# Weight sums of a decoder layer: their transfers on ScalarE's queue, in groups of half-size tiles

## The chip, the cores and the metric

The kernel runs on one core of one Trainium2 chip. The metric is the device time of one execution in microseconds (us). The kernel before took 1721.75 us in the median of three runs (1721.25 to 1722.3).

The engines are named as in the profile: PE is TensorE, DVE is VectorE, ACT is ScalarE, POOL is GpSimd, SP is SyncE. SP does no arithmetic here; it issues transfers, and "SP's queue" is the order in which it issues them. Every engine works through its own instructions in order, and a transfer that an engine issues is one of them.

## The reference, cut to what matters

One decoder layer in float32 with 1024 tokens: two mixers side by side, an output projection, a gated feed-forward network, and a gated embedding at the end.

```python
def forgetting_attention(q, k, v, f_logit, f_bias, q_gain, k_gain):
    ...
    c = jnp.cumsum(logf, axis=1).transpose(0, 2, 1)
    for blk in range(S // FOX_BLOCK):
        ...
        s = jnp.einsum('bhtd,bhsd->bhts', qh[:, :, t0:t1], kh[:, :, :t1]) * scale
        s = s + c[:, :, t0:t1, None] - c[:, :, None, :t1]
        ...
        pr = jax.nn.softmax(s, axis=-1).astype(vh.dtype)
        outs.append(jnp.einsum('bhts,bhsd->bhtd', pr, vh[:, :, :t1]))
...
        x = x + (jax.nn.silu(hf @ w_ffn_gate[layer]) * (hf @ w_ffn_up[layer])) @ w_ffn_down[layer]
```

Two parts matter here: the attention, eight heads of width 64, and the last product, whose weights `w_ffn_down` have 2816 x 1024 elements.

## The kernel before, in words

The stages follow one another: the first mixer (to about 375 us), the attention (about 380 to 760 us), the projections that merge both, the feed-forward network, and the embedding. Float32 products are made of three matmuls each, of a rounded high part and the rest (`xhi`, `xlo`, `whi`, `wlo`; lines 156 to 158 for one shape, 402 to 404 for another).

The attention goes over four pairs of heads, numbered 0 to 3 here, one call of `fox_mix(pr)` each. A pair has two halves. In the first, 24 **score blocks** (two heads, rows in blocks of 128, one or two column ranges) are computed only to find each row's maximum (the reduction of line 871 on DVE). The maxima are transposed on PE (line 879), split into `uh` and `ul` on DVE (lines 882 and 883), and four transfers of line 886 write them into rows 66 to 69 of the operand `QA`. In the second half the scores are computed again with these rows in the contraction, so that they come out with the maximum already subtracted: line 912 on PE needs the transfers of line 886. Then come the exponential on ACT (line 919), its split into `ph` on POOL (line 923) and `pl` on DVE (line 924), and the products with the values. Where the attention leaves PE free, `fill(n)` issues matmuls of projections that are needed later; their results leave PSUM by line 644 on ACT, with line 657 (a square) on ACT, lines 658 to 660 on DVE, line 661 (a power) on POOL, line 666 (the scaling) on DVE and line 669 (the store `qd`) on SP.

The down projection is computed with seven products of sums of blocks in place of eight products of blocks, so it needs four sums of blocks of `w_ffn_down` (S1 to S4) for each of its 11 steps `kp`. `down_sums()` makes these during the attention: for each `kp` it loads four blocks of 128 x 512 (line 789), forms four sums on POOL (line 795), each in the place of one of its operands, and stores them to the DRAM tile `sd` (line 797), from which the down projection loads them much later. `down_sums()` is a generator; `fox_mix` advances it by one step after every score block (line 874), 96 steps in all, so that pairs 0 to 2 have three `kp` each and pair 3 has two. Loads and stores both stand in SP's queue (`dma` is `nc.sync.dma_start`); the tiles come from the pool `wsum` with six buffers.

```python
t[n] = wsum.tile([P, HALF], F32, tag="sw", name="sw")
after_anchor(dma(t[n], wts[U_DOWN + 2 * kp + i][:, b * HALF:(b + 1) * HALF]))
...
    after_anchor(ptt(t[z], t[x], t[y], op))
    yield
    after_anchor(dma(sd[n, kp], t[z]))
```

The order on PE is that of the code. The order on the other engines is set by a scheduler when the program is built; `after_anchor` tells it to place an instruction no earlier than the latest score matmul, which adds no wait on the chip. Transfers report on eight counters in turn (DMAHW0 to DMAHW7): a transfer that takes a counter waits until the one that had it has landed, whichever queue that was issued from.

Of the kernel before, what the change touches and what calls it, by code (L numbers as in the profile page):

```python
# [9 lines left out]
F32 = mybir.dt.float32  # L10
# [4 lines left out]
ALU = mybir.AluOpType  # L15
# [4 lines left out]
P = 128  # L20
# [3 lines left out]
HALF = 512  # L24
D_FF = 2816
NFF = D_FF // P
NPAIR = NFF // 2
# [17 lines left out]
U_DOWN = U_UP + NFF  # L45
# [18 lines left out]
def layer(ctx, tc, xT, pT, wts, wf_in, consts, masks, outT):  # L64
    nc = tc.nc
    dma = nc.sync.dma_start
# [71 lines left out]
    for n, m in GATES_BEFORE:  # L138
        i = order.index(n)
# [145 lines left out]
    for c in range(8):  # L285
        t = w2() if c < 4 else hg.tile([P, HALF], F32, tag=("Kt", "Qt")[c % 2], name="vraw")
# [466 lines left out]
    fstack = ExitStack()  # L753
# [15 lines left out]


    sd = dram.tile([4, NPAIR, P, HALF], F32, name="sd")
    wsum = fstack.enter_context(tc.tile_pool(name="wsum", bufs=6, reuse_waits="tile"))
    S2, S3, S4, S1 = range(4)

    anchor = [None]
# [1 line left out]
    def after_anchor(ins):  # L777

        tc.add_manual_dep(ins.ins, anchor[0].ins.name,
                          mybir.DependencyInfo(mybir.DependencyClass.NoSync,  # L780
                                               mybir.DependencyReason.DATA), reason="order")

    def down_sums():

        for kp in range(NPAIR):
            t = {}
            for n, (i, b) in (("21", (0, 1)), ("22", (1, 1)), ("11", (0, 0)), ("12", (1, 0))):
                t[n] = wsum.tile([P, HALF], F32, tag="sw", name="sw")
                after_anchor(dma(t[n], wts[U_DOWN + 2 * kp + i][:, b * HALF:(b + 1) * HALF]))
            yield  # L790
            yield
            yield
            for x, y, z, op, n in (("21", "22", "22", ALU.add, S1), ("11", "21", "21", ALU.subtract, S3),
                                   ("22", "11", "11", ALU.subtract, S2), ("12", "11", "12", ALU.subtract, S4)):
                after_anchor(ptt(t[z], t[x], t[y], op))  # L795
                yield
                after_anchor(dma(sd[n, kp], t[z]))
            yield

    wsums = down_sums()  # L800
    staged = {}

# [261 lines left out]
    op = ostack.enter_context(tc.tile_pool(name="op", bufs=3, side="right", reuse_waits="tile"))  # L1064
# [267 lines left out]
    for n, (p, kp) in enumerate(todo):  # L1332
# [7 lines left out]
        if n == 2:  # L1340
# [4 lines left out]
                                                 reuse_waits="tile"))  # L1345
# [9 lines left out]
        _, _, g, begin, into, done = products[p]  # L1355
# [129 lines left out]
```

## Time and profile before

| | |
|---|---|
| runs, median (lowest to highest) | 1721.75 us (1721.25 to 1722.3) |
| profiled execution | 1719.14 us, span 1717.4 us |
| PE busy | 1618.3 us, 94% of the span |
| DVE busy | 1088.9 us, 63% |
| ACT busy | 638.7 us, 37% |
| POOL busy | 596.1 us, 35% |
| chain that ended last | PE 85%, DMA 3%, POOL 3%, DVE 3% |
| DMA | 223.45 MB, mean 130 GB/s |

The busy shares are means over all stages. Issuing a transfer is not counted as busy time; in a timeline, SPq is SP's queue, and the time beside an instruction of it is what the issuing took. A releaser (behind "<-") is the event that ended an engine's idle time. PEclk is the clock that TensorE was granted, 1.00 for the full 2.4 GHz and 0.50 for half of it.

### The profile page before, as it was taken

Reading aid. Unit: us, or ns where it says so; the run is one execution under the profiler, and the core shown is the slowest. Engines: PE = TensorE matmul, PEld = TensorE weight load, DVE = VectorE, ACT = ScalarE, POOL = GpSimd, SP = SyncE. Lnnn points to the kernel's source line nnn. Section 1 sums busy time; section 2 is a strip of 40 time slices with the busy share of each in tenths; the row PEclk is TensorE's granted clock in tenths of the full one; section 3 lists DMA queues with packets and bytes.
Section 4 is the critical chain, followed back from the end, with each engine's and each line's share of the span. In section 5 each row is a group of like instructions: output and inputs, shape, how many; then the busy total and the mean of one; then the engine's idle time right before and its main releaser. Section 6 shows DMA issues by size and latency. Waiting matters only on the chain.

```text
span 1717.4 us, 21469 instructions
## 1 busy us (share of the span) xinstructions
PE 1618.3 (94%) x8086; PEld 1356.8 (79%) x8086; DVE 1088.9 (63%) x1431; ACT 638.7 (37%) x888; POOL 596.1 (35%) x452
## 2 busy tenths in 40 slices
PE   8999999997694969799999999999999999999998
PEld 6889889997583847577888888888888878888887
DVE  7457776755462636556547777777777757657442
ACT  7244655632221304156224433333333334445310
POOL 2243444423315233231213466656665620102200
PEclk9999999999796989899999999999999999999999
DMA  5332211246556373707224332223322278665111
GB/s 203 99 113 72 74 62 51 87 139 175 168 146 200 101 227 106 213 33 271 69 101 150 126 104 105 93 92 123 114 96 92 92 253 302 199 193 187 61 64 47
DMA packets 120615, 223.45 MB, mean 130 GB/s; under 512 B 14368, under 2 KB 43424, under 8 KB 120512
## 3 DMA queue, kind: packets, MB, share of 16 engines
q1 hardware_dynamic: 120512, 222.09, 39.4%
q8 instruction: 63, 1.03, 0.2%
q14 instruction: 40, 0.33, 0.1%
HBM read 148.25 MB, written 61.15 MB: 122 GB/s over the span
## 4 chain that ended last, share of the span: by engine, by line
PE 85%; DMA 3%; POOL 3%; DVE 3%; issue 2%; ACT 2%; SPq 1%; POOLq 0%; DVEq 0%; ACTq 0%
PE ps_z L156 14%; PE ps_z L157 14%; PE ps_z L158 14%; PE ps_m L156 6%; PE ps_m L158 6%; PE ps_m L157 6%; POOL sw L795 3%; PE ps_z L402 2%; PE ps_z L403 2%; PE ps_z L404 2%; DMA sw<-wts 1%; PE ps_m L488 1%; PE ps_a L158 1%; PE ps_a L157 1%; PE ps_a L156 1%
## 5 line engine op out<-in xcount | busy, mean ns | idle before, releaser
L156 PE MATMUL ps_z<-xhi,whi 128*128 128x512 f32 x624 | 254.8, 408 | 0.7 <-ACT xhi L173 0.7
L157 PE MATMUL ps_z<-xlo,whi 128*128 128x512 f32 x624 | 245.5, 393 | 0.6 <-DVE xlo L176 0.6
L158 PE MATMUL ps_z<-xhi,wlo 128*128 128x512 f32 x624 | 245.0, 393 | 0.0
L924 DVE TENSOR_TENSOR pl<-p,ph 128x512 fp32r<-128x512 f32 (+3 forms) x96 | 55.4, 583 | 130.7 <-POOL ph L923 130.2
L158 PEld LDWEIGHTS ps_z<-xhi,wlo 128*128 128x128 f32 x624 | 118.1, 189 | 25.2
L1082 DVE TENSOR_TENSOR wlo<-dr,whi 128x1024 fp32r<-128x1024 f32 x75 | 94.9, 1267 | 66.5 <-ACT whi L1081 65.8
L156 PEld LDWEIGHTS ps_z<-xhi,whi 128*128 128x128 f32 x624 | 119.5, 192 | 21.7 <-ACT xhi L173 1.1
L157 PEld LDWEIGHTS ps_z<-xlo,whi 128*128 128x128 f32 x624 | 118.6, 190 | 22.7 <-DVE xlo L176 2.4
L128 ACT CAST whi<-raw 128x1024 fp32r<-128x1024 f32 (+1 forms) x69 | 72.4, 1049 | 153.9 <-PE ps_z L157 119.2
L1081 ACT CAST whi<-dr 128x1024 fp32r<-128x1024 f32 x75 | 79.1, 1055 | 108.7 <-PE ps_m L158 90.0
L129 DVE TENSOR_TENSOR wlo<-raw,whi 128x1024 fp32r<-128x1024 f32 (+1 forms) x69 | 101.6, 1472 | 28.3 <-ACT whi L128 23.8
L402 PE MATMUL ps_z<-whi,xhi 128*128 128x256 f32 (+1 forms) x384 | 112.8, 294 | 0.0
L912 PE MATMUL ps_m<-QA,KA 68*128 68x512 f32 (+3 forms) x96 | 36.2, 377 | 77.0 <-DMA QA<-ul 76.8
L403 PE MATMUL ps_z<-wlo,xhi 128*128 128x256 f32 (+1 forms) x384 | 108.6, 283 | 0.0
L404 PE MATMUL ps_z<-whi,xlo 128*128 128x256 f32 (+1 forms) x384 | 108.5, 283 | 0.0
L919 ACT ACTIVATE p<-ps_m 128x512 f32<-128x512 f32 (+3 forms) x96 | 46.3, 491 | 157.9 <-PE ps_m L915 137.7
L1275 POOL TENSOR_TENSOR w<-w,rb 128x512 f32<-128x512 f32 x44 | 63.0, 1433 | 103.1 <-ACT w L1274 103.1
L923 POOL TENSOR_SCALAR ph<-p 128x512 fp32r<-128x512 f32 (+3 forms) x96 | 53.3, 559 | 126.5 <-ACT p L919 126.4
L1304 POOL TENSOR_TENSOR acc<-acc,o 128x512 f32<-128x512 f32 x14 | 24.6, 1756 | 190.8 <-ACT o L1303 190.1
L795 POOL TENSOR_TENSOR sw<-sw 128x512 f32<-128x512 f32 x44 | 58.3, 1324 | 81.4 <-DMA sw<-wts 78.8
L912 PEld LDWEIGHTS ps_m<-QA,KA 68*128 68x128 f32 x96 | 19.3, 201 | 82.3 <-DMA QA<-uh 54.6
L403 PEld LDWEIGHTS ps_z<-wlo,xhi 128*128 128x128 f32 x384 | 73.3, 191 | 0.7
(462 smaller groups left out, 4518.2 us busy)
## 6 DMA issues: line engine op xcount, KB each, us to landing
raw<-wts SPq DMA_DIRECT2D x71, 512.0 KB
hb<-w SPq DMA_DIRECT2D x77, 256.0 KB
dr<-hb SPq DMA_DIRECT2D x75, 256.0 KB
sw<-wts SPq DMA_DIRECT2D x44, 256.0 KB
sd<-sw SPq DMA_DIRECT2D x44, 256.0 KB
rg<-wts SPq DMA_DIRECT2D x22, 512.0 KB
ru<-wts SPq DMA_DIRECT2D x22, 512.0 KB
dr<-sd SPq DMA_DIRECT2D x44, 256.0 KB
```

What stands on the lines that cost most here:

```text
L128: nc.scalar.copy(hi, raw)
L129: tt(lo, raw, hi.bitcast(F32), ALU.subtract)
L156: mm(ps, w[0], x[0], start=first, stop=False, skip_group_check=more)
L157: mm(ps, w[0], x[1], start=False, stop=False, skip_group_check=more)
L158: mm(ps, w[1], x[0], start=False, stop=last, skip_group_check=more)
L402: mm(ps[:, off:off + n], xh[:, cs], hi, start=k == 0, stop=False)
L403: mm(ps[:, off:off + n], xh[:, cs], lo, start=False, stop=False)
L404: mm(ps[:, off:off + n], xl[:, cs], hi, start=False, stop=k == KT - 1)
L795: after_anchor(ptt(t[z], t[x], t[y], op))
L1081: nc.scalar.copy(hi, src)
L1082: tt(lo, src, hi.bitcast(F32), ALU.subtract)
L1275: ptt(s, s, hv(rb, h), ALU.mult)
```

## The change

Loads and stores of the sums are issued by ACT (`sdma` is `nc.scalar.dma_start`). The work is cut into 22 groups, two for each `kp`, of tiles of 128 x 256 in place of 128 x 512. The pool has twelve such buffers in place of six large ones, the same bytes. Loads of group g + 1 and stores of group g - 1 stand ahead of the sums of group g in the code. 44 loads, 44 sums and 44 stores become 88 of each, all of half the size: 176 transfers of 128 KB in ACT's queue for 88 of 256 KB in SP's.

```diff
-    wsum = fstack.enter_context(tc.tile_pool(name="wsum", bufs=6, reuse_waits="tile"))
+    wsum = fstack.enter_context(tc.tile_pool(name="wsum", bufs=12, reuse_waits="tile"))
...
+    sdma = nc.scalar.dma_start
+    groups = [(kp, q) for kp in range(NPAIR) for q in range(2)]
+
+    def sum_load(kp, q):
+        t = {}
+        for n, (i, b) in (("21", (0, 1)), ("22", (1, 1)), ("11", (0, 0)), ("12", (1, 0))):
+            t[n] = wsum.tile([P, 256], F32, tag="sw", name="sw")
+            c = b * HALF + q * 256
+            after_anchor(sdma(t[n], wts[U_DOWN + 2 * kp + i][:, c:c + 256]))
+        return t
+
     def down_sums():
-        for kp in range(NPAIR):
-            t = {}
-            for n, (i, b) in (("21", (0, 1)), ("22", (1, 1)), ("11", (0, 0)), ("12", (1, 0))):
-                t[n] = wsum.tile([P, HALF], F32, tag="sw", name="sw")
-                after_anchor(dma(t[n], wts[U_DOWN + 2 * kp + i][:, b * HALF:(b + 1) * HALF]))
-            yield
-            yield
-            yield
-            for x, y, z, op, n in (("21", "22", "22", ALU.add, S1), ("11", "21", "21", ALU.subtract, S3),
-                                   ("22", "11", "11", ALU.subtract, S2), ("12", "11", "12", ALU.subtract, S4)):
-                after_anchor(ptt(t[z], t[x], t[y], op))
-                yield
-                after_anchor(dma(sd[n, kp], t[z]))
-            yield
+        t, done = sum_load(*groups[0]), []
+        for _ in range(4):
+            yield
+        for g, (kp, q) in enumerate(groups):
+            for dst, src in done:
+                after_anchor(sdma(dst, src))
+            ahead = sum_load(*groups[g + 1]) if g + 1 < len(groups) else None
+            done = []
+            for x, y, z, op, n in (("21", "22", "22", ALU.add, S1),
+                                   ("11", "21", "21", ALU.subtract, S3),
+                                   ("22", "11", "11", ALU.subtract, S2),
+                                   ("12", "11", "12", ALU.subtract, S4)):
+                after_anchor(ptt(t[z], t[x], t[y], op))
+                done.append((sd[n, kp][:, q * 256:(q + 1) * 256], t[z]))
                 yield
-                after_anchor(dma(sd[n, kp], t[z]))
-            yield
+            t = ahead
+        yield
+        for dst, src in done:
+            after_anchor(sdma(dst, src))
```

In the changed file the load is line 791, the sum line 808, the store line 801 (the last group's line 814); every line from 799 on of the kernel before has moved down by 16, so lines 879, 886, 912, 919 and 923 are lines 895, 902, 928, 935 and 939 there.

The built program shows how the other instructions move. SP's queue at the end of pair 0's first half, before (`raw` is a weight for a projection, `VL`, `zt` and `qd` are the attention's own tiles, and DVE_49, Pool_49 and Activation_49 are waits for those engines):

```order
L789 DMA sw<-wts 128x512 [waits DMAHW3_49,DMAHW0_49]
L669 DMA qd<-zn 128x4x128 [waits DMAHW1_49,DVE_49,Activation_49]
L797 DMA sd<-sw 128x512 [waits Pool_49] x2
L669 DMA qd<-zn 128x4x128 [waits DMAHW4_49]
L797 DMA sd<-sw 128x512 [waits DMAHW5_49,Pool_49]
L797 DMA sd<-sw 128x512 [waits DMAHW6_49,Pool_49]
L886 DMA QA<-uh 1x8x128 [waits DMAHW7_49,DVE_49]
L886 DMA QA<-ul 1x8x128 [waits DMAHW0_49,DVE_49]
L886 DMA QA<-uh 1x8x128 [waits DMAHW1_49]
L886 DMA QA<-ul 1x8x128 [waits DMAHW2_49]
```

The same place after:

```order
L862 DMA VL<-vfd 128x64 [waits DMAHW1_49]
L863 DMA VL<-vfd 128x64 [waits DMAHW3_49]
L864 DMA VL<-vfd 128x7x128 [waits DMAHW5_49]
L669 DMA qd<-zn 128x4x128 [waits DMAHW0_49,DVE_49,Activation_49]
L669 DMA qd<-zn 128x4x128 [waits DMAHW3_49]
L117 DMA raw<-wts 128x1024 [waits DMAHW6_49]
L902 DMA QA<-uh 1x8x128 [waits DMAHW4_49,DVE_49]
L902 DMA QA<-ul 1x8x128 [waits DMAHW1_49,DVE_49]
L902 DMA QA<-uh 1x8x128 [waits DMAHW2_49]
L902 DMA QA<-ul 1x8x128 [waits DMAHW3_49]
```

The stores and loads of the sums no longer stand ahead of the four `QA` transfers. These now come behind two `qd` stores, and wait for counters that were last taken by transfers of ACT's queue: in pair 0 by a load of group 4 and by stores of group 3. In pair 1 they wait likewise for a store of group 8 and a load of group 10; in pair 2 for the second store of group 14, and, through the `raw` load ahead of them, for a load of group 15; in pair 3 for the last store of group 20 and two stores of group 21.

ACT's order from pair 0's first score blocks to its first exponential (line 919), before:

```order
L644 ACTIVATE zn<-ps_z,r_539 128x256 x2
L657 ACTIVATE w_3755<-zn 128x512
L644 ACTIVATE zn<-ps_z,r_539 128x256 x2
L657 ACTIVATE w_3760<-zn 128x512
L644 ACTIVATE zn<-ps_z,r_539 128x256 x2
L657 ACTIVATE w_3962<-zn 128x512
L128 CAST whi<-raw 128x1024
L644 ACTIVATE zn<-ps_z,r_539 128x256 x2
L657 ACTIVATE w_3967<-zn 128x512
L919 ACT_TABLE_LOAD
L919 ACTIVATE p<-ps_m 128x512 x2
```

The same place after, from the second pair of `zn` on, where the exponential is line 935:

```order
L801 DMA sd<-sw 128x256
L657 ACTIVATE w_3771<-zn 128x512
L801 DMA sd<-sw 128x256 x3
L791 DMA sw<-wts 128x256 x4
L801 DMA sd<-sw 128x256 x4
L791 DMA sw<-wts 128x256 x4
L801 DMA sd<-sw 128x256 x4
L791 DMA sw<-wts 128x256 x4
L644 ACTIVATE zn<-ps_z,r_539 128x256 x2
L128 CAST whi<-raw 128x1024
L644 ACTIVATE zn<-ps_z,r_539 128x256 x2
L657 ACTIVATE w_3998<-zn 128x512
```

Before these rows stand 16 more transfers, behind the first pair of `zn` and its square. The third and fourth pairs of `zn`, their squares and a cast of weights (line 128) now stand behind all the transfers of the pair, with the exponential behind them. 40, 48, 48 and 40 transfers stand ahead of the first exponential of pairs 0 to 3. POOL has 20, 24, 24 and 20 half-size sums there, where it had 12, 12, 12 and 8 full ones. In pair 0 its order was two of line 661, one of line 661, four sums, one of line 661, eight sums; it is now one of line 661, twelve sums, one of line 661, eight sums, two of line 661.

## Rows read from the trace of the kernel before

**Rows 1.** Waits of PE, 380 to 780 us; us in total, times, longest.

```profile
PE ps_m L912 <- DMA QA<-ul: 76.8, 4, 23.6
```

**Rows 2.** Timeline of PE: L912's first matmul of each pair; in brackets, idle before.

```profile
443.01 0.80 PE L912 MATMUL ps_m<-QA,KA 68*128 68x512 f32 x1 [23.33 <-DMA QA<-ul]
...
547.32 0.77 PE L912 MATMUL ps_m<-QA,KA 68*128 68x512 f32 x1 [23.62 <-DMA QA<-ul]
...
646.69 0.77 PE L912 MATMUL ps_m<-QA,KA 68*128 68x512 f32 x1 [19.36 <-DMA QA<-ul]
...
727.11 0.77 PE L912 MATMUL ps_m<-QA,KA 68*128 68x512 f32 x1 [10.44 <-DMA QA<-ul]
```

**Rows 3.** Waits of SP's DMA queue, 380 to 780 us; columns as in 1.

```profile
SPq L797 <- POOL sw L795: 92.0, 44, 13.0
```

**Rows 4.** Chain of work, 414 to 444 us; start us, us, what.

```profile
421.57 3.65 DMA sw<-wts
...
441.19 1.77 DMA QA<-ul
```

**Rows 5.** Tile sw: its lines; ns min/median/max, first and last start in us.

```profile
L789 SPq DMA_DIRECT2D sw<-wts x44: 375/426/1067, 400.4 to 714.9; - x44
L795 POOL TENSOR_TENSOR sw<-sw x44: 1259/1262/2147, 414.6 to 722.7; 128x512 f32<-128x512 f32 x44
L797 SPq DMA_DIRECT2D sd<-sw x44: 319/320/744, 415.9 to 723.9; - x44
```

**Rows 6.** Timeline of POOL in pairs 0, 1 and 2; start us, us, instruction.

```profile
395.47 1.64 POOL L661 TENSOR_TENSOR r<-ss,cf 128x8 f32<-128x8 f32 x1 [16.16 <-DVE ss L660]
...
425.35 5.28 POOL L795 TENSOR_TENSOR sw<-sw 128x512 f32<-128x512 f32 x4 [2.57 <-DMA sw<-wts]
434.63 5.28 POOL L795 TENSOR_TENSOR sw<-sw 128x512 f32<-128x512 f32 x4 [3.99 <-DMA sw<-wts]
...
499.47 1.65 POOL L661 TENSOR_TENSOR r<-ss,cf 128x8 f32<-128x8 f32 x1 [13.23 <-DVE ss L660]
...
627.52 5.28 POOL L795 TENSOR_TENSOR sw<-sw 128x512 f32<-128x512 f32 x4 [5.90 <-DMA sw<-wts]
638.24 5.28 POOL L795 TENSOR_TENSOR sw<-sw 128x512 f32<-128x512 f32 x4 [5.44 <-DMA sw<-wts]
```

**Rows 7.** Timeline of SP's queue, pair 0's end and pair 2's start.

```profile
440.35 0.75 SPq L886 DMA_DIRECT2D QA<-uh  x1
...
442.58 0.63 SPq L886 DMA_DIRECT2D QA<-ul  x1
...
599.66 1.24 SPq L840 DMA_DIRECT2D KB<-zt  x1
```

**Rows 8.** Timeline of ACT in pairs 0, 2 and 3.

```profile
416.29 0.84 ACT L644 ACTIVATE zn<-ps_z,r 128x256 f32<-128x256 f32 x2 [0.38 <-PE ps_z L404]
...
595.46 1.05 ACT L128 CAST whi<-raw 128x1024 fp32r<-128x1024 f32 x1 [1.58 <-PE ps_z L157]
...
686.02 0.58 ACT L942 COPY w<-ps_a 64x512 f32<-64x512 f32 x1
```

**Rows 9.** Groups of POOL by form, 380 to 740 us; busy us, mean ns, idle before.

```profile
L923 POOL TENSOR_SCALAR ph<-p 128x512 fp32r<-128x512 f32 x38 | 25.5, 676 | 64.9 <-ACT p L919 64.9
...
L923 POOL TENSOR_SCALAR ph<-p 128x256 fp32r<-128x256 f32 x14 | 6.0, 432 | 12.8 <-ACT p L919 12.8
```

**Rows 10.** Stretches behind the four stops; PEclk is the granted clock.

```profile
443.00:447.20 4.20, 4.19 (x11) 2.77 (x12) 0.69 (x1) 1.02 (x2) 0.62 (x1) 0.50 0.65 182
...
727.10:730.50 3.40, 3.39 (x9) 2.07 (x10) 0.00 (x0) 1.88 (x2) 0.01 (x1) 0.50 0.65 222
sum 18.60, PE 18.56 PEld 12.20 DVE 2.82 ACT 6.22 POOL 3.10; mean PE 4.64 PEld 3.05 DVE 0.70 ACT 1.56 POOL 0.77
```

**Rows 11.** Timeline of DVE around pair 0's stop.

```profile
422.82 0.69 DVE L666 TENSOR_TENSOR zn<-zn,r 128x512 f32<-128x512 f32 x1 [2.95 <-POOL r L661]
...
445.73 0.69 DVE L924 TENSOR_TENSOR pl<-p,ph 128x512 fp32r<-128x512 f32 x1 [22.22 <-POOL ph L923]
```

## The prediction

> **What bounds the kernel now.** The waits of PE come first. PE is busy nearly all the time, so a change elsewhere can only give back time in which PE stands. In the attention stage almost all such time has one cause: four stops, one per pair of heads, at the first score matmul of the second half (line 912), which waits for the maxima to be written into QA. They make 76.8 us [rows 1]. PE's timeline shows each: the idle time in brackets, taken from the start beside it, gives PE's arrival at 419.7, 523.7, 627.3 and 716.7 us [rows 2].
>
> Next, why QA is late. The waits of SP's queue show the store of a sum waiting for POOL 44 times, 92.0 us in all [rows 3]. The QA transfers are issued only at 440.35 in pair 0 [rows 7], though the engine that makes their data (DVE) had been idle for 22 us when it next worked [rows 11]. They stand in SP's queue behind all sums of the pair, and these run in a closed circle: the chain shows a load landing 3.65 us after its issue [rows 4], then four sums of 1.26 us each and four stores [rows 5], and only then the next loads. POOL's timeline gives the length of a circle: 9.28 us in pair 0 (425.35 to 434.63) and 10.72 in pair 2 (627.52 to 638.24) [rows 6]. So the place to look at is the interval from a pair's start to its QA transfers, not POOL's or ACT's share of the span.
>
> The stops cost more than their length. In the stretches behind them the granted clock reads 0.50, which is 1.2 GHz, for 18.6 us of PE work in the four of them together (the first, the last and the sum of four stand in [rows 10]); at 1.00 that work would take half. So 9.3 us more hang on the stops, and 86.1 us can be had at most.
>
> **The change part by part.** *Removed from SP's queue:* 88 issues and the head-of-line wait. If nothing new came in, all 86.1 us would go. What is late next is the new wait of QA for counters held by ACT's transfers, so that chain has to be worked out.
>
> *A half sum.* No row shows one. The nearest is the same engine's copy: 676 ns for 512 columns, 432 for 256 [rows 9], so 188 of it is fixed. With that, 1262 ns [rows 5] becomes 188 + 537 = 0.72 us; I take 0.70. Bounds are half (0.63) and no saving (1.26). Eighty-eight at 0.70 are 61.6 us for today's 44 x 1.32 = 58.3: 3 us more on POOL, under other work.
>
> *The period of a group.* POOL alone would allow 4 x 0.70 = 2.8 us, the lower bound. With loads one group ahead, the loads of g + 1 follow the last store of g - 1: one store issue of 0.32, four load issues of 0.43 [rows 5], a landing of 3.65 [rows 4] and the sums of 2.8 make 8.5 us for two groups, 4.2 each. Half of today's circle, 4.6 us in pairs 0 and 1 and 5.4 in pairs 2 and 3, is near that and holds the load of the other transfers, so I take it. The upper bound is a full trip per group, without overlap: 3.65 + 0.32 + 2.8 = 6.8.
>
> *When QA can be written.* Behind the last sum stand a store's landing, taken as 2.0 us (bounds 1.77 and 3.65, the two landings of rows 4), and the QA transfers, 440.35 to 442.96, 2.6 us [rows 4, 7].
> - Pair 0 needs group 3 stored. POOL is free at 395.47 + 1.64 = 397.1 [rows 6]; 397.1 + 4 x 4.6 + 1.65 for a line 661 in between + 4.6 = 421.8. PE is there at 419.7: 2 us.
> - Pair 1 needs group 8 stored, and group 5 is loaded already: 499.47 + 1.65 = 501.1, + 3 x 4.6 + 1.65 + 4.6 = 521.2 against 523.7. The load of group 10 also gates and comes up to 4 later; I take 1 us.
> - Pair 2 starts when ACT has done its cast, 595.46 + 1.05 = 596.5 [rows 8]: four loads and their landing 5.4, sums 2.8, two periods 10.8, 4.6 make 620.1; through the load of group 15 it is a period and a landing more, 629. PE comes at 627.3; I take 2.
> - Pair 3 starts at 686.02 + 0.58 = 686.6 [rows 8] and has five groups: 686.6 + 5 x 5.4 + 4.6 = 718.2 against 716.7; I take 2.
>
> Left of the waits: 7 us (bounds 0 and 28, the latter by the period of 6.8).
>
> *Behind the wait.* ACT now evicts two quarters of a projection (twice 0.84, twice a square) and makes a cast of 1.05 [rows 8] between the pair's last transfer and its first exponential, and POOL has eight half sums and line 661 twice ahead of `ph`. That was done during the wait before. I take 4 us for pair 0 and 5 for pair 1, none for pairs 2 and 3, where no quarters stand: 9 (bounds 0 and 16, twice 8).
>
> *In the scoring half.* Line 661 on POOL now has up to twelve half sums ahead of it, and DVE's line 666 waits for it; today that wait is 2.95 us [rows 11]. Evictions on ACT wait behind stores that wait for POOL. I take 3 us for each pair, 12 (bounds 0 and 24).
>
> *SP's other transfers* now share counters with ACT's. An issue that is held up takes 1.24 us where others take 0.63 [rows 7]; one late landing is 3.65. I take 1.5 us for each pair, 6 (bounds 0 and 14.6).
>
> *ACT's issuing.* 176 issues. The trace has none on ACT; SP's take 0.32 to 0.43 in the median [rows 5], and the longest near row is 1.24 [rows 7]. I take 0.37, so 40 to 48 of them are 15 to 18 us per pair in stretches of 24 to 31 us (worked out below): no term of its own, because ACT otherwise waits for PE there. If that cover is gone the second rival applies.
>
> *The clock.* Shorter stops remain; I leave half of the 9.3 us lost, 4.7 (bounds 0 and 9.3).
>
> **Sum.** 86.1 - (7 + 9 + 12 + 6 + 4.7) = 47.4 us gained. The profiled execution took 1719.14 us, 2.6 below the median of the runs, so 1671.7 in its terms and **1674 us** in the runs'. All bounds at once would give 1635 (nothing left of the losses) and 1727 (28 + 16 + 24 + 14.6 + 9.3 = 91.9 in place of 38.7). They will hardly all fall to one side, so the likeliest case's own range goes half way to each, 1655 to 1700.
>
> **The rivals.**
> - *The full trip stays.* Stores wait at the head of ACT's queue, ahead of the next loads, so nothing overlaps and a period is 6.8 us. Pair 0 waits 2 + 4 x 2.2 = 11, pair 1 about 4, pair 2 about 4, pair 3 2 + 5 x 1.4 = 9, 28 instead of 7; 4.6 of clock is lost too. That gives about 1700. For it: today's circle is exactly this. Against: twelve buffers are three groups, so the loads of g + 1 need the buffers of g - 2, not of g - 1.
> - *ACT's queue becomes the bound*, on the slow side. Place: the transfers ahead of the first exponential of each pair. From the pairs' starts (395.47 and 499.47 by rows 6, 596.5 and 686.6) to PE's arrivals there are 24 + 24 + 31 + 30 = 109 us. With x us per issue ACT needs 176 x there, and 2 x 0.84 + 1.05 = 2.7 us per pair of evictions and a cast, 11 in all; with 12 us of stalls in scoring it breaks even with the 76.8 of today at x = (109 + 76.8 - 11 - 12) / 176 = 0.92. At 1.0 the kernel is 0.08 x 176 = 14 us slower, **1736 us**. For it: waits for POOL and for counters now lie on an engine that evicts PE's banks, and an issue was seen to take 1.24 when held up. Against: the medians of SP are 0.32 and 0.43, less than half of that point.
> - *Nearly all comes back.* The period is POOL's 2.8 and no stall of scoring appears: only about 7 us are left of the 86.1, so 1719.1 - 79 + 2.6 = 1642.
> - *No change.* Moving transfers between queues does nothing, because the transfers themselves are the limit, and QA is as late as before: 1721. The row that speaks against it is the 92.0 us of a queue's head waiting for POOL, not for a transfer [rows 3]. The Trainium skill says it in "DMA: Bandwidth & Descriptors", section "Issuing engines are not separate DMA queues": transfers of several engines run on the same 16 DMA engines, and issuing from several saves only the sequencer's time to initiate, usually small. By that rule the result would be this rival's; the trace agrees with it on the data's path but shows what it leaves out, a queue whose head waits.
>
> **How the numbers follow.** The forecast gets 0.56, the full trip 0.13, nearly all 0.11, no change 0.05, ACT's queue 0.15. The range leaves out the last two: from 1640 (nearly all) to 1706 (the full trip, with 6 us for its waits). A measurement of this kernel can tell about 0.2%, 3.4 us, from no change. Faster: 0.56 + 0.13 + 0.11 = 0.80; within it 0.05; slower 0.15.
>
> **What the profile of the changed kernel would show.** Right: the waits of PE at line 928 fall from 76.8 to 5 to 25 us, the queue of SP no longer waits for POOL at a sum's store, ACT's queue does, and POOL's sums follow each other every 4 to 5.5 us per group of four. An issue on ACT shows 0.3 to 0.5 us. Full trip: periods near 7 and waits near 28 us. ACT as the bound: issues near 1 us, PE waiting for ACT at score matmuls or for `ph` and `pl`, or long evictions. No change: line 928 still waits some 75 us. I am wrong if waits of the scoring half, which today are small, come to more than 24 us, or if PE's arrival at line 928 moves later by as much as the wait shrinks.

## The result, and the profile after

The changed kernel takes 1684.03 us in the median (1682.1 to 1684.39), the kernel before 1721.5 beside it; the ratio is 0.9782, with a 95% interval of 0.9765 to 0.9799. That is 37 us less. The profiled execution took 1682.1 us, its span is 1680.3.

The waits of PE between 370 and 750 us in the changed kernel (us in total, times, longest) answer to [rows 1]. Lines 916 and 918 are the products with the values, line 895 the transpose of the maxima:

```profile
PE ps_m L928 <- DMA QA<-ul: 17.1, 3, 7.1
PE ps_m L928 <- DMA sw<-wts: 6.1, 1, 6.1
PE ps_a L916 <- POOL ph L939: 6.0, 4, 3.3
PE ps_m L895 <- DVE u L892: 4.3, 1, 4.3
PE ps_a L918 <- DVE pl L940: 3.2, 5, 0.8
```

The first two rows are the four stops at line 928: 17.1 + 6.1 = 23.2 us in place of 76.8. The other three rows are new or larger: PE now waits for `ph`, for `pl`, and once, 4.3 us, for the last maximum. The stops one by one, in the timeline of PE (start us, us, instruction, idle before), stand against [rows 2]:

```profile
426.79 0.80 PE L928 MATMUL ps_m<-QA,KA 68*128 68x512 f32 x1 [6.09 <-DMA sw<-wts]
...
520.50 0.80 PE L928 MATMUL ps_m<-QA,KA 68*128 68x512 f32 x1 [3.98 <-DMA QA<-ul]
...
613.88 0.79 PE L928 MATMUL ps_m<-QA,KA 68*128 68x512 f32 x1 [7.12 <-DMA QA<-ul]
...
689.52 0.77 PE L928 MATMUL ps_m<-QA,KA 68*128 68x512 f32 x1 [5.99 <-DMA QA<-ul]
```

They are 4 to 7 us each, nearly alike, where they were 23, 24, 19 and 10. The profile names the load of a sum as the cause of the first one; the chain below shows what was behind it.

For all kernels of this text the stages can be laid side by side, from the starts of three lines in PE's timeline: a pair's first score matmul (866 before, 882 after), the transpose of the maxima (879, 895), and the first matmul that needs QA (912, 928). "Scoring" is the first to the second, "stop" the second to the third, both summed over four pairs; "behind" is the third to the next pair's first score, over three pairs.

| kernel | scoring | stop | behind | median, us |
|---|---|---|---|---|
| before | 78.7 | 99.9 | 154.7 | 1721.5 |
| changed | 84.0 | 47.6 | 164.1 | 1684.0 |

A stop does not fall to nothing in this counting, since fill work of PE stands in it: in the kernel without sums (below), where PE waits for nothing there, a stop is 5.6 to 5.7 us. The change took 52.3 us from the stops and gave 5.3 back in scoring and 9.4 behind the stops: 37.6 net, of which the rest of the span, 0.5 longer, leaves 37.1, the difference of the two spans.

Why the stops did not fall further is told by the chain of work in pair 0 (start us, us, what):

```profile
402.75 3.99 DMA sw<-wts
...
409.89 2.96 DMA sw<-wts
...
412.93 6.25 DMA qd<-zn
...
419.68 4.67 DMA sd<-sw
```

Two loads, of 3.99 and 2.96 us, then a `qd` store of SP's queue, 6.25 us, then a store of a sum, 4.67 us, and at 424.44 the QA transfer: ACT's store could not be issued before SP's `qd` store gave its counter free, and SP's QA transfer not before ACT's store gave back its own. SP's queue shows the same gap, between the first and the second QA transfer:

```profile
419.92 0.75 SPq L902 DMA_DIRECT2D QA<-uh  x1
424.44 0.66 SPq L902 DMA_DIRECT2D QA<-ul  x1
```

4.5 us lie between them, where 0.84 lay before (440.35 in [rows 7] to 441.19 in [rows 4]).

The group of the tile `sw` (ns min/median/max, first and last start) and POOL's timeline of pair 0 give the sizes:

```profile
L791 ACTq DMA_DIRECT2D sw<-wts x88: 334/455/1607, 393.4 to 677.7; - x88
L808 POOL TENSOR_TENSOR sw<-sw x88: 721/734/1287, 397.0 to 682.9; 128x256 f32<-128x256 f32 x88
L801 ACTq DMA_DIRECT2D sd<-sw x84: 326/390/1443, 398.4 to 682.6; - x84
```

```profile
397.04 6.62 POOL L808 TENSOR_TENSOR sw<-sw 128x256 f32<-128x256 f32 x8
406.87 3.16 POOL L808 TENSOR_TENSOR sw<-sw 128x256 f32<-128x256 f32 x4 [3.21 <-DMA sw<-wts]
...
412.63 3.17 POOL L808 TENSOR_TENSOR sw<-sw 128x256 f32<-128x256 f32 x4 [1.00 <-DMA sw<-wts]
419.98 0.73 POOL L808 TENSOR_TENSOR sw<-sw 128x256 f32<-128x256 f32 x1 [4.18 <-DMA sw<-wts]
423.73 2.32 POOL L808 TENSOR_TENSOR sw<-sw 128x256 f32<-128x256 f32 x3 [3.02 <-DMA sd<-sw]
```

A half sum takes 734 ns. Groups start at 397.04 (two of them in one row), 406.87, 412.63 and 419.98: (419.98 - 397.04) / 4 = 5.7 us a group, with a line 661 of 1.65 us in between (409.98). The fifth group is split, as its second sum waits for a load (issued at 417.76, landed at 423.60, when its counter last rose; the row names a store instead). The sums of the fourth group (group 3, counted from 0), the last whose stores the QA transfers wait for, end at 412.63 + 3.17 = 415.80. In pair 2 the groups are further apart, 6.7 us each over four groups:

```profile
585.85 3.17 POOL L808 TENSOR_TENSOR sw<-sw 128x256 f32<-128x256 f32 x4 [11.97 <-DMA sw<-wts]
...
612.45 3.13 POOL L808 TENSOR_TENSOR sw<-sw 128x256 f32<-128x256 f32 x4 [4.82 <-DMA sd<-sw]
```

An issue on ACT is 455 and 390 ns in the median, up to 1.6 us when held up.

The losses behind the stop are in ACT's and POOL's timelines of pair 0:

```profile
425.51 0.84 ACT L644 ACTIVATE zn<-ps_z,r 128x256 f32<-128x256 f32 x2 [19.27 <-DMA QA<-ul]
...
430.01 1.28 ACT L935 ACT_TABLE_LOAD   x1
```

```profile
430.01 3.25 POOL L661 TENSOR_TENSOR r<-ss,cf 128x8 f32<-128x8 f32 x2 [3.96 <-DVE ss L660]
433.24 1.77 POOL L939 TENSOR_SCALAR ph<-p 128x512 fp32r<-128x512 f32 x2
```

ACT's third quarter of `zn` is evicted only when its last transfers are out (ACT issues the last four loads from 423.62 to 425.41; the QA transfer that the row names stands in SP's queue), and the exponential's table is loaded at 430.01, 3 us after PE had started on the scores (426.79). POOL makes line 661 twice first and begins with `ph` at 433.24.

The loss in scoring is in DVE's timeline of pair 1:

```profile
508.56 0.69 DVE L666 TENSOR_TENSOR zn<-zn,r 128x512 f32<-128x512 f32 x1 [3.38 <-POOL r L661]
```

Line 666 waits 3.38 us for line 661, which stood behind sums on POOL; the last step of the maxima (line 892, at 509.17) stands behind line 666, and the transpose (line 895) waits for that.

The clock came back little. In the stretches behind the four stops the granted clock (the third number from the right) is still near half:

```profile
426.80:431.00 4.20, 4.20 (x12) 2.79 (x13) 2.71 (x5) 4.18 (x7) 0.99 (x1) 0.58 0.76 263
520.50:526.00 5.50, 5.40 (x13) 3.28 (x14) 2.17 (x3) 4.00 (x8) 1.45 (x2) 0.51 0.73 232
613.90:619.50 5.60, 5.60 (x18) 3.80 (x19) 2.01 (x3) 2.66 (x4) 3.54 (x5) 0.63 0.84 248
689.50:693.00 3.50, 3.48 (x10) 2.17 (x10) 0.00 (x0) 1.88 (x2) 0.10 (x1) 0.50 0.78 283
```

(1 - clock) times length, summed, is 4.2 x 0.42 + 5.5 x 0.49 + 5.6 x 0.37 + 3.5 x 0.50 = 8.3 us, where it was 9.3: stops of 4 to 7 us were followed by the lower clock much as those of 10 to 24 us. In pair 1 it fell once more, with the 3.3 us wait for `ph` (line 916):

```profile
529.30:536.10 6.80, 5.57 (x15) 3.97 (x16) 4.71 (x7) 1.36 (x3) 3.60 (x6) 0.50 0.60 193
```

That is 5.57 us of PE's work at 0.50, 2.8 us more, part of the 9.4 behind the stops. So in sum the clock gave nothing back; PE's busy time over the span is 1622.9 us, where it was 1618.3.

### The profile page after: what moved, and what is told of

Same layout as the page of the kernel before. It is cut to its first block, busy times and chain, and to the rows that moved or that the text cites. A ratio compares the mean times of both kernels' runs of the same rounds, so it can differ in the third digit from the quotient of the medians.

```text
span 1680.3 us, 21652 instructions
## 1 busy us (share of the span) xinstructions
PE 1622.9 (97%) x8086; PEld 1359.3 (81%) x8086; DVE 1088.4 (65%) x1431; ACT 637.6 (38%) x888; POOL 604.7 (36%) x496
## 4 chain that ended last, share of the span: by engine, by line
PE 81%; DMA 7%; DVE 4%; issue 3%; ACT 2%; POOL 1%; ACTq 1%; SPq 0%; POOLq 0%; DVEq 0%
PE ps_z L156 14%; PE ps_z L157 14%; PE ps_z L158 13%; PE ps_m L156 6%; PE ps_m L158 6%; PE ps_m L157 6%; DMA sw<-wts 3%; PE ps_z L403 2%; PE ps_z L402 2%; PE ps_z L404 2%; PE ps_m L488 1%; DMA sd<-sw 1%; PE ps_a L157 1%; PE ps_a L156 1%; PE ps_a L158 1%
## 5 line engine op out<-in xcount | busy, mean ns | idle before, releaser
L808 POOL TENSOR_TENSOR sw<-sw 128x256 f32<-128x256 f32 x88 | 65.3, 743 | 74.9 <-DMA sw<-wts 59.4
L402 PEld LDWEIGHTS ps_z<-whi,xhi 128*128 128x128 f32 x384 | 74.1, 193 | 0.1
L404 PEld LDWEIGHTS ps_z<-whi,xlo 128*128 128x128 f32 x384 | 73.6, 192 | 0.0
```

Source lines behind the costliest of these rows:

```text
L402: mm(ps[:, off:off + n], xh[:, cs], hi, start=k == 0, stop=False)
L404: mm(ps[:, off:off + n], xl[:, cs], hi, start=False, stop=k == KT - 1)
```

## The experiments

**Theory 1**, as it stood before the runs: QA is late because a closed circle of load, sums and stores has to turn three times, with everything else of SP's queue behind it; the shorter circle is the gain. **Rival A**: leaving SP's queue is the whole gain. **Rival B**: the queue does not matter, groups and look-ahead do.

### One part of the change alone

*Only the queue*: the code and tiles of before, loads and stores on ACT.

```diff
-                after_anchor(dma(t[n], wts[U_DOWN + 2 * kp + i][:, b * HALF:(b + 1) * HALF]))
+                after_anchor(nc.scalar.dma_start(t[n], wts[U_DOWN + 2 * kp + i][:, b * HALF:(b + 1) * HALF]))
...
-                after_anchor(dma(sd[n, kp], t[z]))
+                after_anchor(nc.scalar.dma_start(sd[n, kp], t[z]))
```

> The kernel before with its full-size tiles and its own schedule; only the queue is ACT's. Theory 1 (the closed circle of load, sums and stores sets when QA can be written, and the queue only decides who else stands behind it): the circle stays at 9 to 11 us, the QA transfers wait for counters of the third group in pairs 0 and 1, and evictions and exponentials now stand behind the stores; the stops of PE at line 912 sum to 30 to 50 us, 15 to 25 us are lost in the scoring half and behind the stops, 1695 to 1715 us. Rival A (leaving SP's queue is the whole gain): 1680 to 1690 us, stops of 15 to 30. Rival B (the queue does not matter, only groups and look-ahead do): 1715 to 1725 us.

*Only the groups*: the changed kernel with its transfers on SP.

```diff
-    sdma = nc.scalar.dma_start
+    sdma = nc.sync.dma_start
```

> The changed kernel with all its groups, but loads and stores on SP's queue. Theory 1: the look-ahead halves the period to 4 to 5 us, so QA comes some 8 us behind PE per pair although it stands behind the sums; nothing is lost on ACT; stops of 30 to 45 us in all, 1675 to 1695 us, close to the changed kernel. Rival A: the stops stay at 60 to 75 us, 1710 to 1725 us. Rival B: the same as the changed kernel within 5 us, with stops as short as its 23 us.

| kernel | scoring | stop | behind | median, us | ratio to before, interval |
|---|---|---|---|---|---|
| only the queue | 98.0 | 40.0 | 159.3 | 1683.4 | 0.978 (0.9758 to 0.9801) |
| only the groups | 79.2 | 83.4 | 154.1 | 1702.2 | 0.9898 (0.9878 to 0.9917) |

The queue alone gives the whole 38 us, as Rival A said, and theory 1 missed it by some 12 us. The groups alone give 19, less than theory 1 expected and more than Rival A. Together they give no more than the queue alone. PE's waits of the first (columns as above):

```profile
PE ps_m L912 <- DMA QA<-ul: 16.8, 4, 9.6
PE ps_m L866 <- DVE u L871: 13.8, 4, 7.5
```

and its POOL timeline of pair 0:

```profile
400.90 5.38 POOL L795 TENSOR_TENSOR sw<-sw 128x512 f32<-128x512 f32 x4 [3.75 <-DMA sw<-wts]
413.54 5.28 POOL L795 TENSOR_TENSOR sw<-sw 128x512 f32<-128x512 f32 x4 [7.26 <-DMA sw<-wts]
418.79 1.64 POOL L661 TENSOR_TENSOR r<-ss,cf 128x8 f32<-128x8 f32 x1
425.55 5.40 POOL L795 TENSOR_TENSOR sw<-sw 128x512 f32<-128x512 f32 x4 [5.12 <-DMA sw<-wts]
```

The circle did not get shorter here, it is 12.6 and 12.0 us. But it begins earlier: the first sum is at 400.90, where it was 414.6 [rows 5]. Two things differ. SP's queue had issued the loads only behind the pair's operand loads, from 400.4 [rows 5]. And the scheduler's order on POOL had put a line 661, which waits for DVE, ahead of the sums:

```profile
413.01 1.64 POOL L661 TENSOR_TENSOR r<-ss,cf 128x8 f32<-128x8 f32 x1 [7.43 <-DVE ss L660]
```

By their counters the two loads that the first sum needs had landed by 405.7, so 9 of the 13.7 us are POOL's order, which moved along when the queue was changed. No run varies that order by itself; how much of the 38 us hangs on it stays open. On the other side the score matmuls (line 866) wait 13.8 us for DVE to give a bank back; line 661 on POOL, on which DVE's line 666 waits, now stands behind eight sums. The groups' run has the waits of PE, of SP's queue and the tile's sums as follows:

```profile
PE ps_m L928 <- DMA QA<-ul: 60.2, 4, 18.5
```

```profile
SPq L801 <- POOL sw L808: 27.1, 23, 10.8
```

```profile
L808 POOL TENSOR_TENSOR sw<-sw x88: 721/722/1636, 414.6 to 706.5; 128x256 f32<-128x256 f32 x88
```

The head of SP's queue waits 27.1 us for POOL instead of 92.0 [rows 3], so the circle is broken; but the first sum is at 414.6 again, behind the same line 661, and QA stands behind the sums' transfers: 60.2 us of stops. So theory 1 became **theory 1a**: the queue's gain is an earlier start of the sums and that QA stands behind nothing which waits for POOL.

### The QA transfers alone

The kernel before, with only the four QA transfers of a pair moved.

```diff
-                dma(fb(QA[a][66 + i:67 + i]), fb(t[a * 8:a * 8 + 8]))
+                nc.scalar.dma_start(fb(QA[a][66 + i:67 + i]), fb(t[a * 8:a * 8 + 8]))
```

> The kernel before, with only the four QA transfers of each pair issued by ACT. The sums keep queue, size and circle. Theory 1 (head of line in SP's queue): the wait of line 912 for QA falls from 76.8 to under 15 us, but POOL's copy to ph then stands behind the same circle of sums, so part of the time returns as waits for ph; 1680 to 1705 us. Rival A' (the QA transfers are late because the DMA engines are busy): stops of 60 us and more, 1710 to 1725 us. Rival C (nothing else stands behind the sums): 1635 to 1650 us.

1680.7 us, ratio 0.9768 (0.975 to 0.9786), at the lower edge of what theory 1 had; scoring 78.7, stop 23.2, behind 187.3. PE's waits:

```profile
PE ps_a L900 <- POOL ph L923: 26.7, 9, 5.9
PE ps_a L902 <- DVE pl L924: 5.0, 9, 1.0
PE ps_m L912 <- DMA QA<-ul: 2.3, 2, 2.0
```

The stops are gone (2.3 us), though the sums keep their queue, size and circle: in the kernel before, the lateness of QA was the head of SP's queue and nothing else. But 187.3 - 154.7 = 32.6 us come back behind the stop, much of it as waits for `ph` (26.7) and `pl` (5.0). A move of sixteen small transfers gives as much as the whole change.

### No sums

The kernel before without loads, sums and stores in the attention; the down projection loads single blocks of the weight in their place.

```diff
-                    next(wsums, None)
+                    pass
...
-    summed = lambda kp, i: sd[i, kp]
+    summed = lambda kp, i: block_of(kp, i % 2, i // 2)
```

> The kernel before without the sums: no loads, sums and stores in the attention; the down projection loads single blocks of the weight where it had loaded sums, so its output is another. Theory 1: all four stops go, with the half clock behind them: 1633 to 1645 us, the most that any placing of the sums can give. Rival: if something else is late at line 912, stops of 10 us and more remain and the time stays above 1650 us.

1634.1 us, ratio 0.9496 (0.9481 to 0.9512): scoring 78.6, stop 22.6, behind 148.3. No stop is left among PE's waits of the attention; the largest is:

```profile
PE ps_a L902 <- DVE pl L924: 2.5, 6, 0.8
```

So the sums cost the kernel before 87 us, and the changed kernel still 50. PE's busy time here is 1609.2 us, 9.1 less than before, which agrees with the 9.3 that the prediction put down to the clock.

### Loads and stores on different queues

> The changed kernel with its loads back on SP's queue; the stores stay on ACT's. Theory 1a (the gain of the queue is that the sums start some 7 to 13 us earlier and that QA stands behind no store that waits for POOL): the sums start late again, as loads stand behind the pair's QB, KB and VL transfers, but QA has only loads in front; stops of 25 to 45 us, little lost on ACT; 1680 to 1695 us. Rival (what matters is that SP's queue waits for no sum): 1665 to 1680 us, stops below 23.

```diff
-            after_anchor(sdma(t[n], wts[U_DOWN + 2 * kp + i][:, c:c + 256]))
+            after_anchor(dma(t[n], wts[U_DOWN + 2 * kp + i][:, c:c + 256]))
```

> The changed kernel with its stores back on SP's queue; the loads stay on ACT's. Theory 1a: the sums start as early as in the changed kernel and ACT no longer waits for POOL, so the losses in the scoring half and behind the stops (15 us in the changed kernel) fall to 3 to 8; QA stands behind the stores of the pair's groups, so the stops are 15 to 35 us; 1665 to 1685 us. Rival (a queue whose head waits for POOL is the cost): stops of 50 us and more, 1700 us and more.

```diff
-            after_anchor(sdma(dst, src))
+            after_anchor(dma(dst, src))
...
-        for dst, src in done:
-            after_anchor(sdma(dst, src))
+        for dst, src in done:
+            after_anchor(dma(dst, src))
```

| kernel | scoring | stop | behind | median, us | ratio to before, interval |
|---|---|---|---|---|---|
| loads on SP | 79.2 | 75.2 | 155.7 | 1694.5 | 0.9851 (0.9833 to 0.9869) |
| stores on SP | 85.5 | 68.2 | 156.3 | 1694.0 | 0.9849 (0.9828 to 0.9869) |

Both took 10 us more than the changed kernel. Theory 1a had the loads' run near the upper end of its time, with longer stops than it expected (the first sum is at 414.6 again, with its loads issued from 400.4), and missed the stores' run by 9 us: the sums started early there (397.8 us), and yet PE waited 45.0 us at the stops. Loads on SP, the wait of PE and that of SP's queue:

```profile
PE ps_m L928 <- DMA QA<-ul: 52.0, 4, 14.6
```

```profile
SPq L791 <- DMA sd<-sw: 34.0, 23, 10.2
```

Stores on SP:

```profile
PE ps_m L928 <- DMA QA<-ul: 45.0, 4, 14.1
```

```profile
SPq L801 <- DMA sw<-wts: 26.9, 13, 7.6
```

Here SP's loads wait 34.0 us for ACT's stores (for a buffer or a counter), and SP's stores wait 26.9 us for ACT's loads, which they do not use: that is the shared counter. So whichever half is left in SP's queue holds its head, and QA behind it. On ACT both halves cost less in stops and more behind them: 164.1 against 156. That the losses behind the stop come from ACT's transfers agrees with these three rows; it was not separated further.

### The sums in the second half of a pair

These runs move the call that advances the sums from the score blocks to the blocks behind the stop. The first has the code of before otherwise, the second that of the change, the third that of the change on SP's queue.

```diff
-                    next(wsums, None)
...
-                    mm(ps[:, 0:n], KA[a][0:68, sb], QA[a][0:68, t0:t1], start=True, stop=False)
+                    anchor[0] = mm(ps[:, 0:n], KA[a][0:68, sb], QA[a][0:68, t0:t1], start=True, stop=False)
...
+                    next(wsums, None)
                     fill(0.87)
```

> The kernel before with queue, size and order of the sums kept, but advanced once per block of the second half instead of the first, so that no sum stands ahead of the QA transfers. Theory 1: all four stops go (under 3 us in all); POOL carries 1.3 us of sum beside 0.3 to 0.7 of ph per block of about 2 us, which costs 0 to 15 us of waits for ph; 1634 to 1652 us, near the bound without sums (1634). Rival D (the circle moves into the second half and holds ph or SP's other transfers as it held QA): 1665 to 1700 us.

> The changed kernel, ACT's queue and groups, likewise advanced in the second half. Theory 1: the stops go as well; ACT's exponentials, one per block, stand behind stores that wait for POOL and for counters, 5 to 20 us; 1640 to 1660 us, no better than the same on SP's queue. Rival A (ACT's queue is the better place anywhere): 1630 to 1640 us and faster than on SP's queue.

> The changed kernel's groups on SP's queue, advanced in the second half. Against the run with full-size sums on SP's queue (1665 us; 31 us lost to waits for ph and pl and what follows them) a sum holds POOL for 0.73 us in place of 1.29. Theory 1 (the loss there is ph standing behind a sum on POOL): the loss falls by a third to a half, 1648 to 1660 us. Rival (the loss is something else, such as the transfers or the order): 1662 to 1680 us. Against the same groups on ACT's queue (1675 us) it is faster by 10 to 25 us, if exponentials standing behind stores cost that there.

| kernel | scoring | stop | behind | median, us | ratio to before, interval |
|---|---|---|---|---|---|
| full size, SP | 78.7 | 22.6 | 176.3 | 1665.4 | 0.9676 (0.9655 to 0.9696) |
| groups, ACT | 78.7 | 22.6 | 175.8 | 1674.7 | 0.973 (0.9704 to 0.9756) |
| groups, SP | 78.7 | 22.6 | 166.2 | 1653.6 | 0.9613 (0.9591 to 0.9635) |

In all three the stops are as short as without sums, on either queue: the QA transfers then take counters which only transfers of SP's queue had. What remains is behind: 28, 27.5 and 18 us more than without sums. The first run was slower than theory 1 expected (1652 at most) and hit the lower edge of its rival. Its largest waits of PE, and those of the third run (lines 901 and 917 are the same, 899 and 915 too):

```profile
PE ps_a L901 <- DVE pl L923: 9.2, 15, 2.6
PE ps_a L899 <- POOL ph L922: 5.7, 5, 2.5
```

```profile
PE ps_a L917 <- DVE pl L939: 6.1, 17, 0.8
...
PE ps_a L915 <- POOL ph L938: 3.5, 7, 1.1
```

With half-size sums the loss falls from 28 to 18 us, as expected if `ph` stands behind a sum on POOL. Waits are only half of it. The span of the first run is 32 us longer than without sums; PE's waits between 380 and 760 us make 16 of them (20.8 against 4.9), and PE's busy time is longer by as much (1625.4 against 1609.2), at a mean granted clock of 0.992 against 0.999. In the third run it is 1620.0 us at 0.996. On ACT's queue the exponentials themselves wait:

```profile
ACT p L934 <- DMA sw<-wts: 31.6, 10, 5.9
...
ACT p L934 <- POOL sw L808: 12.7, 5, 3.4
```

31.6 us for loads and 12.7 for POOL, and the second run ends 15 us above what theory 1 expected at most. So the same groups cost 21 us more on ACT's queue than on SP's (1674.7 against 1653.6; the execution in the table is the fastest of its four, 1669.4) once QA does not stand behind them; which queue is better depends on who is behind it.

### Three attempts on the rest

*Full size on SP's queue, spread over the pairs* (four kp in pairs 0 and 1, one in pair 2, two in pair 3):

```diff
-                    next(wsums, None)
+                    for _ in range((1 + (count % 3 == 0), 1 + (count % 3 == 0), count % 3 == 0, count % 3 > 0)[pr]):
+                        next(wsums, None)
```

> The second-half version with full-size sums on SP's queue, with four steps kp in pairs 0 and 1, one in pair 2 and two in pair 3, as pair 2 lost most (14 us against the kernel without sums, pairs 0 and 1 lost 6 and 8), having no matmuls to fill with. Theory 1: pair 2's loss falls to about 5 us, pairs 0 and 1 grow by 2 to 3 each; 1658 to 1664 us. Rival (the loss goes with the number of sums wherever they stand): 1665 us, no change.

1660.0 us, ratio 0.965 (0.9632 to 0.9667); pair 2 behind the stop took 45.5 us instead of 56.8, pairs 0 and 1 together 125.0 instead of 119.5. Theory 1 held.

*Groups on SP's queue, one block more between exponential and product*, with eight buffers:

```diff
-        LAG = 3
+        LAG = 4
...
-    wsum = fstack.enter_context(tc.tile_pool(name="wsum", bufs=12, reuse_waits="tile"))
+    wsum = fstack.enter_context(tc.tile_pool(name="wsum", bufs=8, reuse_waits="tile"))
...
-                    ph = fx.tile([P, HALF], R, tag="ph", bufs=3, name="ph")
-                    pl = fx.tile([P, HALF], R, tag="pl", bufs=3, name="pl")
+                    ph = fx.tile([P, HALF], R, tag="ph", bufs=4, name="ph")
+                    pl = fx.tile([P, HALF], R, tag="pl", bufs=4, name="pl")
```

> The groups on SP's queue in the second half, with eight buffers in place of twelve, and the products with the values one block later behind their exponential (four blocks instead of three, four ph and pl buffers). Theory 1 (the loss is latency of ph and pl, not POOL's throughput): more of it is hidden, 1640 to 1655 us, 4 us or more below the run without it. Rival (throughput of POOL and DVE): no difference to that run within 3 us.

1657.4 us, ratio 0.9636 (0.9621 to 0.965): 4 us more, not less. Two things changed at once (buffers and distance), so the run says only that this is no gain.

*Groups on SP's queue, spread over the pairs* (32 steps in pairs 0 and 1, 8 in pair 2, 24 in pair 3):

```diff
-                    next(wsums, None)
+                    for _ in range((1 + (count % 3 == 0), 1 + (count % 3 == 0), count % 3 == 0, 1)[pr]):
+                        next(wsums, None)
```

> The groups on SP's queue in the second half (1653.6 us), with their steps spread over the pairs as in the run with full-size sums: 32 in pairs 0 and 1, 8 in pair 2, 24 in pair 3. That spread took 11 us from pair 2 and gave 6 back in pairs 0 and 1 there. Theory 1: pair 2, which still loses 10 us against the kernel without sums, loses 2 to 4; pairs 0 and 1 lose 2 to 4 more together; 1645 to 1652 us. Rival (half-size sums leave nothing for the spread to gain): 1652 to 1657 us.

1654.9 us, ratio 0.9627 (0.9614 to 0.9641): no change against 1653.6, as its rival had it. Behind the stop pair 2 gave 8.3 us (52.9 to 44.6), pairs 0 and 1 took 5.7 back, and pair 2's stop 1.8. The best kernel of this study is the groups on SP's queue, advanced in the second half: 1653.6 us, 30 us below the changed kernel.

## Why the prediction was right, and where its sizes were off

The forecast was faster, 1674 us in a range of 1640 to 1706; measured are 1684. Direction and mechanism held: four stops behind one queue, with 86.1 us to be had at most; the kernel without sums shows 87. The terms that were left of these 86.1:

| term | taken, us | measured, us | where |
|---|---|---|---|
| stops | 7 (0 to 28) | 23.2 | PE's waits at line 928 |
| behind the wait | 9 (0 to 16) | 10.4 | 9.4 by the stages, less the clock's -1.0 |
| scoring half, SP's others | 12 + 6 (0 to 38.6) | 5.3 | scoring, 84.0 - 78.7 |
| clock | 4.7 (0 to 9.3) | 8.3 | granted clock behind the stops |
| sum | 38.7 | 47.2 | |

The measured terms leave 86.1 - 47.2 = 38.9 us, the spans differ by 37.1. The term that was off most is the **stops**: 7 us taken, 23.2 measured, inside the bound of 28. The clock took 3.6 us more than its term and the loss behind the wait 1.4, while scoring and SP's others took 12.7 less; that the sum came within 10 us is in part luck.

The step that failed is "when QA can be written", and pair 0 shows where. The working had the sums of the fourth group end at 397.1 + 4 x 4.6 + 1.65 = 417.2 and QA written 4.6 us later, at 421.8. The sums ended at 415.80, before that; the matmul that needs QA started at 426.79, 11.0 us behind the last sum.

- *The counters.* The prediction named them and gave them 1.5 us a pair outside the stops. They act inside, twice: the first store of the fourth group was issued at 419.25, 3.45 us after the last sum, when SP's `qd` store had given its counter back; and the second QA transfer was issued 4.5 us after the first, when a sum's store had landed. The runs with the sums in the second half, where QA follows no transfer of a sum, have no stops on either queue; no run changes the counters alone.
- *The landing of a store.* 2.0 was taken, from the nearer of two rows (1.77, a transfer of a few rows), with 3.65 as the upper bound; 4.67 was measured. For the kernel before 2.0 would have been right: by their counters its 44 stores landed in 1.97 us in the median, and the 88 half-size ones of the changed kernel in 4.07 (in 2.70 where the groups stay on SP's queue). The row was of the wrong kernel: it could not show a landing with both queues at work.
- *The period.* In pair 0, up to the fourth group, it held: (412.63 - 397.04 - 1.65) / 3 = 4.6 us, the 4.6 that was taken. In pair 2, where 5.4 was taken, it is 6.7, outside the 4 to 5.5 us that the prediction named as its sign. The working gave a landing of 3.65 to the loads only and let nothing of SP's queue into the circle; in the chain of pair 0 a `qd` store of 6.25 us stands ahead of ACT's stores.

The two terms in scoring and on SP were set too high, 18 for 5.3, and hid most of that. POOL's line 661 did stall the scores, in pairs 0 and 1 only (1.1 and 5.0 us), by the mechanism given. The term behind the wait was right in size and place; 2.8 us of it are the second fall of the clock in pair 1, of which the prediction has nothing. ACT's issue was taken as 0.37 us and is 0.46 and 0.39, well under the 0.92 from which the slow rival would have decided; ACT as a bound did not come. With the waits between them it was nearer: the 40 transfers of pair 0 held ACT's queue from 393.4 to 425.4, 0.8 us each.

The "full trip" rival (6.8 us a period, 28 us of stops, 1700) is nearer than the forecast to the measured stops and to the period of pair 2; the measured time lies between the two, nearer to the forecast. "Nearly all" (1642 us) was reached by no run that makes the sums; the best took 1653.6. The rival of no change is answered by two runs: with only the queue of the sums changed 38 us went, with only the QA transfers moved 41. The rule of the Trainium skill named there ("DMA: Bandwidth & Descriptors", section "Issuing engines are not separate DMA queues") agrees with the landings, which did not get shorter on the second queue (3.99 and 4.67 us in the chain above, 3.65 in [rows 4]), and not with the time: what the second queue saved was not the issuing but the waiting of one queue's head. That the trace of before agreed with it on the data's path, as the prediction says, could not be read there: SP issued all 730 transfers of the program. The prediction took the groups and look-ahead for the core of the change; the first two runs show that the queue alone, with the order on POOL that came with it, gives the same time, by an earlier start, and the groups alone half of it.

## What to carry to other kernels

When one queue issues both transfers that wait for an engine and transfers on which another engine waits, look at the head of that queue, and first move the few urgent ones away or the slow ones to a place in the program where nothing urgent follows: sixteen QA transfers on another queue gave as much as the whole change, and advancing half-size sums behind the stop 66 us. Before moving transfers to a computing engine's queue, list what stands behind them there and which counters they share with the old queue. A price for a landing is to be taken from a row of the same size under the same load; a row of the kernel before does not have the load of the kernel after, and where there is no other, the dear end is the better centre for a chain that holds several of them.

## What was not expected of the hardware

In the chain shown, transfers of 128 KB on ACT's queue beside SP's took 2.96 to 4.67 us to land, around the 3.65 us of 256 KB before: half the size did not halve them. By the counters of all the sums' transfers, loads landed in 4.52 us in the median before and 3.98 after, stores in 1.97 and 4.07; with the same half size all on SP's queue it was 2.92 and 2.70. What made them longer with both queues at work was not separated. After stops of 4.0 to 7.1 us the granted clock was 0.50 to 0.63 in the next 3.5 to 5.6 us, close to the 0.50 after stops of 10.4 to 23.6 us, so shortening a stop to some 5 us gave back only 1.0 of 9.3 us, and a new wait of 3.3 us, with 6.8 us at 0.50 around and behind it, cost 2.8.
